# A bank copied out at once and planned durations revised in a one-core two-layer decoder kernel

## The chip, the cores and the metric

The kernel runs on one core of a Trainium2 chip. The metric is device time in microseconds (us) from launch to end of one execution; lower is better. Before the change the median of three runs is 806.67 us (804.53, 806.67, 809.62).

The engines of the core have short names: PE is the matrix engine (PEld is its weight load), DVE the vector engine, ACT the scalar engine, POOL the general-purpose engine, SP the queue that issues most of the transfers. Each engine works through its own queue in order.

## What is computed

The reference is a decoder trunk of two layers on 512 tokens of width 1024, all in float32. The change touches layer 0 alone, whose mixer is a recurrence over tokens with 16 heads of 64:

```python
xmix = xn[None] + (x_prev - xn)[None] * mu[:, None, None, :]
rkvg = jnp.einsum('cbsd,cde->cbse', xmix[:4], w_in)
...
decay = jnp.exp(-jnp.exp(-jax.nn.softplus(-w_pre) - 0.5))
a = jax.nn.sigmoid((a0 + (xa @ a1) @ a2).astype(f32))
...
kk = k * k_k.astype(f32).reshape(H, N)
kk = kk / jnp.maximum(jnp.linalg.norm(kk, axis=-1, keepdims=True), 1e-12)
k = k * (1.0 + (a - 1.0) * k_a.astype(f32).reshape(H, N))

def step(state, inp):
    r_t, w_t, k_t, v_t, kk_t, a_t = inp
    s_kk = jnp.einsum('bhij,bhj->bhi', state, kk_t)
    state = (state * w_t[:, :, None, :]
             - s_kk[..., None] * (kk_t * a_t)[:, :, None, :]
             + v_t[..., None] * k_t[:, :, None, :])
    return state, jnp.einsum('bhij,bhj->bhi', state, r_t)
```

Its output is normalised per head, gated and projected. Every layer ends with a gated embedding that is added to the residual. Layer 1 is causal differential attention with a gate, over one shared set of keys and values.

## The kernel before

**Matmuls in three passes.** Every large product is a float32 product made of three fast ones: an operand is split in a rounded high part and the rest, and `mm3` (lines 283 to 286) multiplies high by high, high by rest and rest by high. So lines 284, 285 and 286 carry all dense products. A weight tile is loaded as a pair into a RAW buffer and split in `w_split` (line 303): the rounding copy (line 269, a helper called from many places, on ACT or DVE) and the subtraction (line 317, on POOL or DVE).

**Stages of layer 0.** A dense half is a product of 1024 inputs by 512 outputs, 32 groups of three matmuls, into four PSUM banks. `ORDER` names them: r, k and v for the first half of the channels, r, k and v for the second half, half of the embedding's product p, both halves of the gate g, the rest of p. In `dense_m` the loop over the eight input tiles is the outer one and that over the four output tiles the inner one, so the four banks are taken at the first input tile and are all finished with the last. The mixed inputs are made by `mix` (lines 529 ACT, 531 DVE, 535 ACT, 537 DVE) the first time a kind is needed, and read back from DRAM the second time.

**Keys.** As an output tile i of the key half ends, `k_evac(i, pk)` (line 845) takes over its bank `pk`. It waits for `("decay", i)`, squares the bank on ACT into an H tile (line 855, for the norms), multiplies it on DVE into three operands K, A and B that the decay stage has prepared (lines 859, 861, and `scaled`, lines 722 and 725), and then gives the bank back. The norms need the squares of four tiles: `head_sums` (a product at line 812, a copy at 817, transposes at 823), the reciprocal at 833, the spread of the norms at 869 and 874. After that the operands are complete and `gram` may form its products (line 964 PE, 973 DVE).

**Decay.** `decay(i)` runs for even and odd tiles as two streams. It takes one R tile, two H tiles and banks, makes two products (lines 737 and 738), three exponentials on ACT (775, 777, 779), a running sum on DVE (771) and some merges, the last of which is on POOL (794).

**Inverse and recursion.** `inverse` solves small triangular systems by 31 steps of two DVE operations (lines 1031 and 1034), with transposes (1022, 1040, 1055), merges (1051, 1059), small copies (line 269 with 32 partitions, 1095) and small products (1067, 1081). `recur` then runs eight steps per half of the channels: products with the state (1168, 1181, 1209), half-copies of 64 x 256 elements (line 269), and the new state on DVE (1221, 1224). `finish` normalises and gates what it yields, after which the output product may start.

**What sets the order.** All these are generators that run in a planner, `Streams`, when the kernel is built. Each `yield` names an engine and a planned duration; `"ACT/DVE"` lets the planner choose the engine that ends first (a later-named one only if it ends 0.15 us earlier), a `!` means that the next step of the same stream need not wait for this one, and a `+` that the step holds a resource that DVE and POOL share in the plan. For PE a second number is the share of its columns. The planner always issues the step that can start first by its own clock, and steps of a better priority first among equals. The sequence so found is the order of every engine's queue on the chip: nothing is reordered later, and a step that is not ready holds up all behind it.

Buffers are counted too. `take` and `free` count four banks of the kind "pd" (dense products) and four of the kind "pw" (all else), 42 R tiles and 11 H tiles of SBUF, 8 weight tiles, 2 RAW buffers and 2 mixed tiles per stream. A tile of the kind H is 128 x 512 or a little more.

```python
            t = max(x[1] + lat, self.clock.get(eng, 0.0), self.port if port else 0.0)
            if best is None or t + w + PREF < best[0] + best[2]:
                best = (t, eng, w, port)
```

## Time and profile before

| what | value |
|---|---|
| median of three runs | 806.67 us |
| the profiled execution, its own time | 804.9 us |
| its span, first to last instruction | 803.1 us |
| mean granted PE clock | 0.987 |

The profile is of one execution. Its span leaves out what lies around the first and the last instruction (804.9 - 803.1 = 1.8 us). In the rows of the timeline the columns are start, length, engine, line, operation, output and inputs by the program's names, and the count of equal instructions; in brackets stands how long the engine was idle before and what released it. In rows of groups the busy time, the mean in ns and the idle time before them stand behind the bars. In rows by stretches each engine's busy time is followed by its count of instructions. A row of the waits reads: who waited, for whom, the sum in us, how often, and the longest.

### The profile page before, as it was taken

How to read it: one execution, taken by the hardware profiler on the slowest of the kernel's cores; microseconds unless marked ns; L12 is line 12 of the kernel's file. 1: busy time of each engine (PE TensorE's matmuls, PEld its weight loads, DVE VectorE, ACT ScalarE, POOL GpSimd, SP SyncE). 2: the span in 40 equal slices, each digit the busy share in tenths (PEclk: the TensorE clock that was granted, in tenths of full speed). 3: DMA queues.
4: the chain of work that ended last, by engine and by line, in shares of the span. 5: the costliest groups of instructions: out<-in, count | busy, mean ns of one | idle time of the engine just before them, and what ended most of it. 6: DMA issues, size and time to landing. Idle time of an engine off the chain costs nothing.

```text
span 803.1 us, 13885 instructions
## 1 busy us (share of the span) xinstructions
PE 757.5 (94%) x5016; PEld 605.5 (75%) x5016; DVE 590.5 (74%) x1354; ACT 453.2 (56%) x1082; POOL 200.2 (25%) x219
## 2 busy tenths in 40 slices
PE   6898899997899879999999999999999999999996
PEld 3676578876677657887778888887888878888884
DVE  2999999988759887788867675446874668835844
ACT  3789754668646555656444564333764467743431
POOL 2406405321504423886210020000000002100000
PEclk9999999999999969999999999999999999999999
DMA  8586667722326768656357434587943334224702
GB/s 322 205 277 217 226 242 267 261 92 92 120 85 227 253 215 288 196 183 198 124 171 262 131 132 134 181 302 219 289 172 105 100 85 145 85 74 157 258 6 105
DMA packets 65525, 144.60 MB, mean 180 GB/s; under 512 B 6448, under 2 KB 27184, under 8 KB 65456
## 3 DMA queue, kind: packets, MB, share of 16 engines
q1 hardware_dynamic: 42672, 108.06, 40.0%
q10 hardware_dynamic: 22784, 35.66, 12.9%
q8 instruction: 39, 0.64, 0.3%
q14 instruction: 30, 0.25, 0.1%
HBM read 105.94 MB, written 37.75 MB: 179 GB/s over the span
## 4 chain that ended last, share of the span: by engine, by line
PE 64%; DVE 17%; DMA 8%; ACT 6%; issue 3%; POOL 1%; SPq 1%; ACTq 0%; DVEq 0%; POOLq 0%
PE p L284 16%; PE p L286 15%; PE p L285 15%; PE p L1168 2%; PE p L964 2%; PE p L1768 2%; DMA RAW<-in_b_w_in 2%; DVE p L1034 2%; DVE H L1031 1%; DVE R L317 1%; PE p L1181 1%; ACT R L269 1%; DMA R<-bD 1%; PE p L1733 1%; PE p L1732 1%
## 5 line engine op out<-in xcount | busy, mean ns | idle before, releaser
L284 PE MATMUL p<-R,R 128*128 128x512 f32 x800 | 327.4, 409 | 8.4 <-ACT R L535 7.4
L285 PE MATMUL p<-R,R 128*128 128x512 f32 x800 | 314.0, 393 | 4.1 <-DVE R L537 4.1
L286 PE MATMUL p<-R,R 128*128 128x512 f32 x800 | 314.3, 393 | 0.0
L284 PEld LDWEIGHTS p<-R,R 128*128 128x128 f32 x800 | 151.2, 189 | 42.3 <-ACT R L535 9.3
L285 PEld LDWEIGHTS p<-R,R 128*128 128x128 f32 x800 | 151.5, 189 | 32.8 <-DVE R L537 6.0
L286 PEld LDWEIGHTS p<-R,R 128*128 128x128 f32 x800 | 151.0, 189 | 33.0 <-DVE R L1298 0.4
L317 POOL TENSOR_TENSOR R<-RAW,R 128x512 fp32r<-128x512 f32 x50 | 67.9, 1363 | 159.6 <-ACT R L269 86.3
L269 ACT CAST R<-RAW 128x512 fp32r<-128x512 f32 x107 | 63.9, 620 | 15.8 <-DMA RAW<-in_w_k 7.2
L317 DVE TENSOR_TENSOR R<-RAW,R 128x512 fp32r<-128x512 f32 x90 | 62.1, 704 | 12.2 <-ACT R L269 11.2
L323 DVE SCALAR_TENSOR_TENSOR R<-RAW,vec,R 128x512 fp32r<-128x512 f32 x64 | 46.5, 748 | 17.4 <-ACT R L321 16.9
L321 ACT ACTIVATE R<-RAW,vec 128x512 fp32r<-128x512 f32 x64 | 44.6, 721 | 20.2 <-DMA RAW<-in_b_w_in 12.8
L1377 POOL TENSOR_TENSOR hr<-hm,half 128x1 f32<-128x1 f32 x16 | 10.5, 656 | 147.0 <-DVE hm L1375 147.0
L1744 ACT ACTIVATE H<-p,mx 128x128 f32<-128x128 f32 (+3 forms) x64 | 33.4, 527 | 21.4 <-DVE mx L1741 20.6
L1737 DVE CUSTOM_DVE_ANT_0 p<-p,cmask 128x128 f32<-128x128 f32 (+3 forms) x64 | 30.4, 510 | 14.6 <-PE p L1733 14.4
L1034 DVE TENSOR_TENSOR p<-p,H 128x126 f32<-128x126 f32 (+22 forms) x124 | 32.6, 263 | 4.3
L280 POOL TENSOR_TENSOR orr<-orm,half 128x4 f32<-128x4 f32 x8 | 8.8, 1101 | 106.6 <-DVE orm L278 93.1
L1031 DVE TENSOR_TENSOR H<-p,R 128x126 f32<-128x126 f32 (+22 forms) x124 | 30.7, 248 | 1.1
L529 ACT ACTIVATE p<-R,omm 128x512 f32<-128x512 f32 x32 | 22.1, 692 | 13.0 <-DVE R L973 5.8
L1514 DVE SCALAR_TENSOR_TENSOR R<-H,R 128x512 f32<-128x512 f32 x16 | 11.1, 692 | 24.4 <-ACT H L1507 22.5
L1507 ACT ACTIVATE H<-p 128x512 f32<-128x512 f32 x16 | 9.5, 596 | 31.1 <-PE p L286 31.1
L1436 ACT COPY R<-p 128x512 f32<-128x512 f32 x16 | 9.4, 586 | 30.7 <-PE p L286 30.5
L1694 POOL MEMSET R<- 64x1024 f32 x8 | 7.6, 949 | 74.9 <-DMA kvD<-R 34.5
(221 smaller groups left out, 1285.1 us busy)
## 6 DMA issues: line engine op xcount, KB each, us to landing
mD<-R ACTq DMA_DIRECT2D x32, 512.0 KB, 3.9
R<-mD SPq DMA_DIRECT2D x32, 512.0 KB, 5.3
RAW<-in_ple_gate SPq DMA_DIRECT2D x16, 512.0 KB, 3.8
RAW<-in_kv_w SPq DMA_DIRECT2D x16, 512.0 KB, 3.8
RAW<-in_b_w_in SPq DMA_DIRECT2D x16, 512.0 KB, 4.3
R<-bD ACTq DMA_DIRECT2D x24, 256.0 KB, 5.6
R<-in_x SPq DMA_DIRECT2D x8, 512.0 KB, 6.1
RAW<-in_w_r SPq DMA_DIRECT2D x8, 512.0 KB, 3.8
```

The costliest lines, as they stand in the source:

```text
L269: (nc.scalar.copy if sc.eng == "ACT" else ENG[sc.eng].tensor_copy)(dst, src)
L284: nc.tensor.matmul(ps, ah, bh, start=first, stop=False)
L285: nc.tensor.matmul(ps, ah, bl, start=False, stop=False)
L286: nc.tensor.matmul(ps, al, bh, start=False, stop=last)
L317: ENG[sc.eng].tensor_sub(lo, f, hi.bitcast(F32))
L321: nc.scalar.activation(hi, f, AF.Copy, scale=g)
L323: nc.vector.scalar_tensor_tensor(lo, f, g, hi.bitcast(F32), ALU.mult, ALU.subtract)
L529: nc.scalar.activation(m, x_at(d), AF.Copy, scale=omm[:, c, d : d + 1])
L1031: ve.tensor_mul(tmp[:, 0:m, 0:w], bc(xs[:, s_ : s_ + 1, 0:w], [P, m, w]), bc(nb[:, s_ + 1 : 32, s_ : s_ + 1], [P, m, w]))
L1034: ve.tensor_add(xs[:, s_ + 1 : 32, 0:w], xs[:, s_ + 1 : 32, 0:w], tmp[:, 0:m, 0:w])
L1737: nc.vector.tensor_tensor_reduce(scs[m][:, 0:n], scs[m][:, 0:n], cmask[:, S - n : S], 1.0, -3.0e38, ALU.add, ALU.max, mx[:, m : m + 1])
L1744: nc.scalar.activation(E[m][:, 0:n], scs[m][:, 0:n], AF.Exp, bias=mx[:, m : m + 1], scale=0.125, accum_out=sm[:, m : m + 1])
```

## The change

The change edits `k_evac` and 17 planned durations. In `k_evac` the wait for the decay moves behind the square, and for the second half (tiles 4 to 7, `g == 1`) ACT copies the bank into an H tile, gives the bank back, and the three DVE operations read the copy. The other edits alter only numbers that the planner uses, and at two places the `!` of a half-copy's first part goes, which lets the plan's second part wait for the first. No priority and no count of buffers is altered.

```diff
                 if scale is None:
-                    yield "ACT/DVE+", (0.52, 0.34)
+                    yield "ACT/DVE+", (0.55, 0.45)
                     copy(hi, f)
...
-            yield "ACT", 0.57
+            yield "ACT", 0.63
             nc.scalar.activation(m, x_at(d), AF.Copy, scale=omm[:, c, d : d + 1])
...
-        yield "ACT!", 0.5
+        yield "ACT!", 0.62
         nc.scalar.activation(A, pfv[:, :, :, 0:64], AF.Exp, scale=-0.5 * DECAY)
-        yield "ACT!", 0.5
+        yield "ACT!", 0.65
         nc.scalar.activation(pf, pf, AF.Exp, scale=-0.5 * DECAY)
...
-        yield "PE", 0.95, 0.25
+        yield "PE", 1.25, 0.25
         for q in range(4):
             nc.tensor.matmul(pn[32 * q : 32 * q + 32], hsel, SQ[what, 4 * g + q], start=True, stop=True)
...
             yield "spawn", bonus(g), EVP["k"]
-        yield "wait", ("decay", i)
         yield "take", "H", 1
         sq = SQ["sq", i] = HT([P, S])
         yield "ACT", 0.57
         nc.scalar.activation(sq, pk, AF.Square, scale=vcol(V_KK, i))
         yield "set", ("sq", i)
+        if g == 1:
+            yield "take", "H", 1
+            kc = HT([P, S])
+            yield "ACT", 0.58
+            nc.scalar.copy(kc, pk)
+            yield "free", "pd", 1
+            pk = kc
+        yield "wait", ("decay", i)
         K, B, A = parts(i)
...
         scaled(i, B, v4(pk), der[:, 4, i : i + 1], B, ALU.mult)
-        yield "free", "pd", 1
+        yield ("free", "H", 1) if g == 1 else ("free", "pd", 1)
...
-                    yield "ACT/DVE+!", (0.2, 0.2)
+                    yield "ACT/DVE+!", (0.31, 0.25)
                     copy(four(na[r, 8 * u + 4 * hh : 8 * u + 4 * hh + 4]), lower(q, u, hh)[:, :, :, 32 * (q % 2) : 32 * (q % 2) + 32])
...
-        yield "PE", 1.67, 0.5
+        yield "PE", 1.15, 0.7
...
             for x in range(2):
-                yield "ACT/DVE!" if x == 0 else "ACT/DVE", (0.3, 0.35)
+                yield "ACT/DVE", (0.37, 0.4)
                 copy(tiles_of(gt, x)[HALF[par][x]], tiles_of(pA, x)[HALF[par][x]])
...
-                yield "ACT!", 0.3
+                yield "ACT!", 0.38
                 nc.scalar.copy(tiles_of(yT, x)[HALF[par][1]], tiles_of(pA, x)[HALF[par][1 - x]])
...
-        yield "Pool+", 1.0
+        yield "Pool+", 1.25
         nc.gpsimd.tensor_add(wg, wg, bc(vmean[:, cq, 8 * g : 8 * g + 8].unsqueeze(2), [P, 8, HN]))
...
-        yield "Pool+/DVE+", (1.0, 0.6)
+        yield "Pool+/DVE+", (1.25, 0.64)
         ENG[sc.eng].tensor_mul(yg, yg, bc(rs.unsqueeze(2), [P, 8, HN]))
```

The same numbers are set at the sister steps: the second small product and the copies back in `inverse`, the second pair of half-copies in `recur`, the second POOL step and the other two merges in `finish`.

More of the change, by code (lines that the diff above doesn't have):

```diff
@@ L1076, in inverse @@
         ps = [bank("pw") for _ in range(2)]
-        yield "PE", 1.67, 0.5
+        yield "PE", 1.15, 0.7
         for hd in range(16):
@@ L1087, in inverse @@
                 for q in range(4):
-                    yield "ACT/DVE+!", (0.2, 0.2)
+                    yield "ACT/DVE+!", (0.31, 0.25)
                     copy(lower(q, u, hh)[:, :, :, 32 * (q % 2) : 32 * (q % 2) + 32], four(xm[quads[q], sl]))
@@ L1199, in recur @@
             for x in range(2):
-                yield "ACT/DVE!" if x == 0 else "ACT/DVE", (0.3, 0.35)
+                yield "ACT/DVE", (0.37, 0.4)
                 copy(tiles_of(uv, x)[HALF[par][x]], tiles_of(pA, x)[HALF[par][x]])
@@ L1250, in finish @@
         bb = bon[:, cq, 4 * g : 4 * g + 4, :].rearrange("p a b -> p (a b)").unsqueeze(2)
-        yield "Pool+", 1.0
+        yield "Pool+", 1.25
         nc.gpsimd.tensor_add(wg, wg, bc(vmean[:, cq, 8 * g : 8 * g + 8].unsqueeze(2), [P, 8, HN]))
-        yield "Pool+", 1.0
+        yield "Pool+", 1.25
         nc.gpsimd.tensor_mul(wg, wg, bc(bb, [P, 8, HN]))
@@ L1266, in finish @@
         rs = yield from rsqrt(ax, s2, 1.0 / HN, GN_EPS, 8, "grs")
-        yield "Pool+/DVE+", (1.0, 0.6)
+        yield "Pool+/DVE+", (1.25, 0.64)
         ENG[sc.eng].tensor_mul(yg, yg, bc(rs.unsqueeze(2), [P, 8, HN]))
         yield "wait", ("lnxg",)
-        yield "Pool+/DVE+", (1.0, 0.6)
+        yield "Pool+/DVE+", (1.25, 0.64)
         ENG[sc.eng].tensor_mul(y, y, lnxg[0][:, gsl])
-        yield "Pool+/DVE+", (1.0, 0.6)
+        yield "Pool+/DVE+", (1.25, 0.64)
         ENG[sc.eng].tensor_add(y, y, w)
```

## The prediction

> **What bounds the kernel now.** I read the page's head and busy table first, then the table by stretches, then who waits for whom inside the poor stretches, then the timeline there. The busy table:
>
> ```profile
> span 803.1 us, 13885 instructions
> PE 757.5 (94%) x5016; PEld 605.5 (75%) x5016; DVE 590.5 (74%) x1354; ACT 453.2 (56%) x1082; POOL 200.2 (25%) x219
> PE 64%; DVE 17%; DMA 8%; ACT 6%; issue 3%; POOL 1%; SPq 1%; ACTq 0%; DVEq 0%; POOLq 0%
> ```
>
> TensorE is busy for 94% of the span and carries 64% of the chain that ended last, so what can be gained is its idle time and the time in which its clock was down. The table by stretches (length, busy time of PE, PEld, DVE, ACT and POOL, granted clock, DMA share, GB/s) tells where that is:
>
> ```profile
> core 0: us, PE busy (x) PEld busy (x) DVE busy (x) ACT busy (x) POOL busy (x), PEclk, DMA share, GB/s
> 20.00:160.00 140.00, 131.15 (x773) 99.44 (x773) 132.59 (x283) 98.56 (x203) 53.26 (x53) 1.00 0.68 243
> 184.00:216.00 32.00, 24.35 (x307) 17.99 (x306) 26.14 (x44) 24.47 (x65) 13.49 (x17) 0.95 0.34 112
> 216.00:245.00 29.00, 29.00 (x300) 22.20 (x299) 19.39 (x40) 13.81 (x38) 3.11 (x3) 1.00 0.35 112
> 245.00:275.00 30.00, 29.46 (x150) 23.60 (x150) 27.44 (x88) 19.14 (x43) 14.46 (x15) 1.00 0.78 275
> 275.00:300.00 25.00, 17.84 (x176) 13.36 (x175) 23.91 (x64) 15.20 (x41) 7.09 (x6) 0.73 0.51 185
> 300.00:420.00 120.00, 117.13 (x1087) 93.35 (x1086) 91.83 (x190) 67.14 (x168) 61.33 (x60) 1.00 0.58 195
> 420.00:803.00 383.00, 372.43 (x1845) 310.65 (x1843) 243.12 (x586) 191.45 (x474) 36.12 (x40) 1.00 0.47 154
> ```
>
> Two stretches stand out. From 184 to 216 PE is idle for 32.0 - 24.35 = 7.65 us with a clock of 0.95; from 275 to 300 it is idle for 25.0 - 17.84 = 7.16 us with a clock of 0.73. Clock loss is (1 - clock) x busy: 0.05 x 24.35 = 1.2 us and 0.27 x 17.84 = 4.8 us. Together 20.8 us. From 20 to 160 PE loses another 8.85 us in small pieces while VectorE is at 132.59 of 140; the copies are not there and I count nothing on it. After 300 PE stands at 98% and 97%, and from 216 to 245 at 100%: there nothing is to be had, and a delay there costs in full. VectorE is the second bound: 27.44 of 30 and 23.91 of 25 us between 245 and 300, but only 19.39 of 29 between 216 and 245. Inside the first stretch, PE waited for these, and these were the steps of the second half's keys (k_evac for tiles 4 to 7):
>
> ```profile
> PE p L874 <- ACT H L869: 2.2, 1, 2.2
> PE p L1181 <- DVE R L1224: 1.8, 2, 1.6
> PE p L1209 <- ACT H L754: 1.6, 1, 1.6
> PE p L1209 <- ACT R L269: 1.0, 1, 1.0
> 186.23 1.26 ACT L855 ACTIVATE H<-p,vec 128x512 f32<-128x512 f32 x2
> 204.39 0.68 ACT L855 ACTIVATE H<-p,vec 128x512 f32<-128x512 f32 x1
> 207.03 0.69 DVE L859 TENSOR_TENSOR R<-p,R 128x512 f32<-128x512 f32 x1
> 193.30 0.47 PE L284 MATMUL p<-R,R 128*128 128x512 f32 x1
> 208.84 0.47 PE L284 MATMUL p<-R,R 128*128 128x512 f32 x1
> 199.11 1.16 PE L1181 MATMUL p<-R,R 128*128 128x128 f32 x8 [1.56 <-DVE R L1224]
> 207.05 1.16 PE L1181 MATMUL p<-R,R 128*128 128x128 f32 x8 [0.28 <-DVE R L1224]
> 219.56 1.16 PE L964 MATMUL p<-R,R 64*128 64x128 f32 x16
> ```
>
> None of these waits is for the matmul stream (L284 to L286) itself; PE waits at the head of its queue for steps of the recursion and of the keys, with no matmul of the value half issued ahead of them. That half takes its four banks only as the keys' tiles give theirs back: its first matmul stands at 193.30, and groups are still scarce at 208.84. A tile gives its bank back after its three merges, and these wait for that tile's decay. The squares (L855) wait for it too: two at 186.23, the last at 204.39, which puts the key norms and so the Gram products (L964, of this half first at 219.56) behind it.
>
> **The change part by part.** *The copy of the bank* (k_evac, tiles 4 to 7). The wait for the decay moves behind the square; four copies of 128x512 from PSUM by ACT are added; three merges per tile then read SBUF; the bank goes free after the copy, and one H tile more is held until the merges are done. No DMA is moved and nothing passes SP's or POOL's queue. The prices and the matmuls of the stretch:
>
> ```profile
> L1481 ACT COPY H<-p 128x512 f32<-128x512 f32 x16 | 9.4, 589 | 9.2 <-PE p L286 9.2
> L284 PE MATMUL p<-R,R 128*128 128x512 f32 x5 | 2.4, 485 | 0.0
> L861 DVE TENSOR_TENSOR R<-p,R 128x512 f32<-128x512 f32 x4 | 2.7, 682 | 0.0
> 183.10 0.43 DVE L269 CAST R<-RAW 128x512 fp32r<-128x512 f32 x1
> 199.84 0.60 ACT L269 CAST R<-RAW 128x512 fp32r<-128x512 f32 x1
> ```
>
> The copy is the L1481 form, 589 ns, so 4 x 0.589 = 2.4 us more on ACT. ACT has 32.0 - 24.47 = 7.5 us idle in the stretch, which covers it; if the cover is gone the copies stand ahead of the recursion's small copies and cost up to 2.4 us. I take 0 and keep 0 to 2.4. The merges stay at 682 ns (L861); that they read SBUF is priced with the port below.
>
> What it brings: the banks come free after square and copy, whose four pairs take about 4 x (0.68 + 0.59) = 5 us of ACT from 186 on, so by about 191 instead of one by one until about 209. Weights are at hand: the value half's last cast before the gap stands at 183.10 and the next at 199.84, and at least three of its eight weight tiles are rounded by then (I count three), each good for four groups of three matmuls. A group takes 0.70 us (rows of the second stall below). That is 12 groups ready against 5 which ran in the stretch (L284 x5), so 7 x 0.70 = 4.9 us of matmuls can move into the 7.65 us of idle. With them goes the same share of the clock loss, 4.9 / 7.65 x 1.2 = 0.8. First term: 5.7 us. Lower end 5.7 - 2.4 = 3.3 with the copies on the path, or nothing if the time comes back later (a rival); upper end all of 8.85, since a consumed weight tile gives its buffers back and lets the next be rounded. The key norms move too, from behind 204.39 to about 191, so the 2.2 us wait of L874 for L869 should go; it lies inside the same 7.65 and isn't counted twice. What is late next is the decay of tile 7 itself, then the recursion's steps (L1181 after L1224).
>
> *The planned durations.* They issue no instruction; they change which engine a step of the slashed kind goes to and in what order all queues stand. How far the old numbers were off, and the second stall:
>
> ```profile
> L269 ACT COPY H<-R x53: 282/297/298, 99.3 to 275.9; 32x128 f32<-32x128 f32 x53
> L269 ACT CAST R<-RAW x107: 601/619/669, 19.3 to 770.7; 128x512 fp32r<-128x512 f32 x107
> L269 DVE CAST R<-RAW x33: 406/421/3389, 50.8 to 759.1; 128x512 fp32r<-128x512 f32 x33
> L529 ACT ACTIVATE p<-R,omm 128x512 f32<-128x512 f32 x32 | 22.1, 692 | 13.0 <-DVE R L973 5.8
> 276.23 0.40 PE L284 MATMUL p<-R,R 128*128 128x512 f32 x1
> 276.93 0.39 PE L284 MATMUL p<-R,R 128*128 128x512 f32 x1
> 276.29 2.08 DVE L1022 STREAM_TRANSPOSE R<-H 128x1024 f32<-128x1024 f32 x1
> 280.60 1.69 DVE L1059 TENSOR_TENSOR H<-H,unit 128x512 f32<-128x512 f32 x1
> 282.59 0.75 DVE L531 SCALAR_TENSOR_TENSOR p<-R,vec,p 128x511 f32<-128x511 f32 x1
> 284.06 0.79 PE L284 MATMUL p<-R,R 128*128 128x512 f32 x1 [5.61 <-ACT R L535]
> 278.37 5.05 POOL L317 TENSOR_TENSOR R<-RAW,R 128x512 fp32r<-128x512 f32 x3 [7.24 <-ACT R L269]
> ```
>
> The small merges of the inverse were planned at 0.20 us and took 297 ns on ACT: over these 53 alone the plan was short by 53 x 0.097 = 5.1 us. The mixing step L529 was planned at 0.57 and took 692 ns, 32 x 0.122 = 3.9 us more. Where a plan is short, an in-order queue holds a step that isn't ready ahead of one that is. The second stall looks like that: L1022 starts at 276.29, behind ACT's small copies, and L531, which PE waits for through L535 (5.61 us, row 284.06), comes only after the inverse's DVE chain at 282.59. With copies planned at 0.31 the mixing step may be put ahead. The prize is 7.16 + 4.8 = 12.0 us. But VectorE is busy there for 23.91 of 25 us, so it is only partly an error of order. From both sides: all 12.0 gone, or a second stall of the same kind elsewhere, 12.0 lost. I take a quarter, 3.0: VectorE's own idle time just before (9.6 us from 216 to 245) says that its work can move forward once the Gram products come earlier, the 96% says that not much can. The cast of a weight tile tips slightly towards ACT (0.55 against 0.45 where it was 0.52 against 0.34): 421 ns of DVE become 619 of ACT for a few of 33; nothing counted. The second half-copy of a recursion step now waits for the first in the plan, as the longer durations of the groupwise merges do theirs after 300: PE is at 98% there; nothing counted.
>
> Of this the clock bears one rule. The Trainium skill ("TensorE: Matmul & The Clock Gate", Part 1) says that an idle window of about 3.4 us halves the clock; by it only the gap of 5.61 us would cost clock time, and the gaps of the first stretch, 2.2 us at most each, would cost none, which would make the first term 4.9. The granted clock of 0.95 in that stretch speaks for a little loss there all the same.
>
> **The sum.** This profiled execution took 804.9 us (span 803.1). 804.9 - 5.7 - 3.0 = 796.2. The median of the three runs, 806.7, is 1.8 above this execution, so against the median: 798.0.
>
> **The rivals.** *The stall goes as a whole* (12.0 instead of 3.0): 806.7 - 5.7 - 12.0 = 789. For it: L531 needs nothing from the inverse. Against: VectorE at 96%. *The gain is absorbed*: the value half ends earlier and PE then stands in front of the gate half, whose operands VectorE makes at 91 to 96% load between 245 and 300; of 5.7 some 2 are left: 804.5. For it: that load. Against: 9.6 us of idle VectorE from 216 to 245 which earlier Gram products can fill. *The port*: the merges were of one PSUM and one SBUF operand, now of two in SBUF. Row 280.60 shows such an operation (L1059) at 1.69 us beside POOL's L317 (three in 5.05 us), where L861 takes 0.68, about 1.0 us more. POOL is busy for 13.49 of 32 us in the stretch, so of twelve merges some five meet it, five us of DVE, half of them on the path: 798.0 + 2.5 = 800.5. The Trainium skill ("SBUF — State Buffer", two separate sides) states the rule: a VectorE operation with two SBUF inputs and a GpSimd operation that reads SBUF lock each other out for a whole instruction; the row of L1059 agrees. *Slower: the H tiles run out.* There are 11. Four squares and four copies hold 8, the inverse 4 until its last copies, a decay 2 each. If the last two decays wait for H, the decay of tile 7 comes one recursion step later, about 8 us (L1181 runs once a step: 199.11, 207.05), the Gram products with it, and PE, which has no slack from 216 on, loses most of that: 806.7 + 6 = 813. It decides from the point at which 219.56 is not reached earlier than now. Against it: the four squares are given back at about 192 then, not after 204.39. A new order that sets a stall like that of 284.06 elsewhere costs the same kind of sum and is counted with it.
>
> **How the numbers follow.** Forecast 0.40 (own range 791 to 802, of it 0.28 below 798.6), the stall gone 0.14, absorbed 0.23, the port 0.05, H or a new stall 0.18. About 1% (8 us) is what a measurement of this kernel can tell from no change. Faster by more: 0.28 + 0.14 = 0.42; within: 0.12 + 0.23 + 0.05 = 0.40; slower: 0.18. The range 787 to 812 leaves out the best end of the stall and the larger half of the slow case.
>
> **What would show it.** Right: the second half's squares all stand within some 6 us of the end of the key matmuls; more than 5 of L284 between them and the first L964 of that half, which comes before 215; PE idle in that stretch under 4 us. The second term: a gap before L284 behind L535 of under 4 us and a clock over 0.85 there. Wrong: the copies standing ahead of the recursion's copies on ACT; merges of over 1 us beside POOL; a new gap of PE above 3 us anywhere between 20 and 420; or the first L964 no earlier than 219.

## The result and the profile after

The changed kernel takes 818.45 us in the median of four runs (814.91 to 820.14) where the kernel before takes 806.46 (804.53 to 809.62) beside it. The ratio is 1.0149, with a 95% interval of 1.0122 to 1.0176: slower, by about 12 us. The forecast was 798.0 with a range of 787 to 812, and the chance that had been given to slower was 0.18. The profiled execution of the changed kernel took 820.14 us, with a span of 818.3.

In the lines of the changed kernel, every number from 857 on is 7 higher: the square L855 is L854, since the wait ahead of it is gone, and L860 is new, the copy of the bank; L859 is L866, L964 is L971, L973 is L980, L1067 is L1074, L1181 is L1188, L1298 is L1305. The head of its page and the busy times:

```profile
span 818.3 us, 13890 instructions
PE 766.5 (94%) x5016; PEld 610.5 (75%) x5016; DVE 597.0 (73%) x1359; ACT 460.9 (56%) x1088; POOL 190.1 (23%) x212
```

These say almost nothing: the same count of matmuls, the same 94%. Three rows of the table by stretches, with the boundaries of the table before (length, busy time of PE, PEld, DVE, ACT and POOL, granted clock, DMA share, GB/s):

```profile
20.00:160.00 140.00, 128.71 (x691) 96.16 (x691) 128.97 (x264) 93.69 (x185) 53.46 (x53) 0.98 0.67 237
184.00:216.00 32.00, 23.41 (x328) 18.47 (x327) 24.08 (x43) 23.77 (x66) 9.61 (x12) 0.84 0.18 59
275.00:300.00 25.00, 15.90 (x71) 11.45 (x70) 18.44 (x49) 11.31 (x26) 3.82 (x3) 0.80 0.59 216
```

Neither poor stretch got better. From 184 to 216 PE is idle for 8.6 us (7.65 before) and its clock fell from 0.95 to 0.84; from 275 to 300 it is idle for 9.1 us (7.16 before), at a clock of 0.80 (0.73). By the prediction's own sum, idle time plus (1 - clock) x busy, the first stretch loses 12.3 us (8.9 before) and the second 12.3 (12.0). From 20 to 160, where the prediction counted nothing, PE lost 2.4 us of busy time and some clock. The timeline of the changed kernel shows what the copies did (start, length, engine, line, operation):

```profile
183.43 0.69 ACT L854 ACTIVATE H<-p,vec 128x512 f32<-128x512 f32 x1
184.53 0.59 ACT L860 COPY H<-p 128x512 f32<-128x512 f32 x1
191.97 1.25 ACT L854 ACTIVATE H<-p,vec 128x512 f32<-128x512 f32 x2
207.21 0.59 ACT L860 COPY H<-p 128x512 f32<-128x512 f32 x1
205.29 1.12 PE L1216 MATMUL p<-R,R 128*64 128x64 f32 x16 [3.59 <-ACT R L1102]
213.60 1.24 DVE L771 TENSOR_TENSOR_SCAN H<-scanm,H 128x520 f32<-128x520 f32 x1
230.71 1.16 PE L971 MATMUL p<-R,R 64*128 64x128 f32 x16
282.08 0.76 PE L284 MATMUL p<-R,R 128*128 128x512 f32 x1 [4.33 <-ACT R L535]
293.96 0.50 PE L284 MATMUL p<-R,R 128*128 128x512 f32 x1 [3.48 <-ACT R L535]
```

The squares are done at 193 instead of 205, as the change means them to be. But the copies stand at 184.53, 187.37, 195.44 and 207.21: the last bank comes free at 207.8, hardly before the 209.1 of the kernel before, and six dense groups stand between 184 and 216 where five stood. PE's longest wait there is now one of 3.59 us for copies of an inverse (L1102). The last running sum of the decays (L771) starts at 213.60, where it had started at 196.0, and the first Gram product of the second half stands at 230.71 instead of 219.56. The stall behind L535 is still there, as two waits of 4.33 and 3.48 us instead of one of 5.61. The copies cost what they had been priced at, and so did ten of the twelve merges that now read SBUF (groups of the changed kernel):

```profile
L866 DVE TENSOR_TENSOR R<-H,R 128x512 f32<-128x512 f32 x4 | 2.7, 687 | 0.5 <-ACT H L860 0.5
L860 ACT COPY H<-p 128x512 f32<-128x512 f32 x4 | 2.4, 594 | 0.0
```

The third merge of a tile, L722, took 1.67 and 1.39 us in two tiles, each time beside an operation of POOL; before, two of this line at 191.53 and 200.96 took 0.75 and 0.74:

```profile
186.40 3.01 POOL L794 TENSOR_TENSOR R<-R,H 128x512 f32<-128x512 f32 x2 [12.09 <-ACT H L779]
188.29 1.67 DVE L722 SCALAR_TENSOR_TENSOR R<-H,der,R 128x512 f32<-128x512 f32 x1
199.24 2.88 POOL L890 TENSOR_TENSOR H<-R,R 128x512 f32<-128x512 f32 x2 [0.41 <-PE p L1088]
201.27 1.39 DVE L722 SCALAR_TENSOR_TENSOR R<-H,der,R 128x512 f32<-128x512 f32 x1
```

The time is lost by *when* things run, so the useful reading is a table of milestones: the start of the first matmul of a dense group (a group is one L284 with its L285 and L286; 800 of them, numbered from 0), and of the last L1298, the last operation of `finish` on what layer 0's output product reads. All from the traces, in us, as the distance to the kernel before; the last six columns are kernels of the experiments below. Each column is one execution: that of the change was 1.7 us above its median and that of before 1.6 us below, so the last row says 15.2 where the medians differ by 12.

| milestone | before | change | bank copy alone (e1) | exponentials (e9) | head sums (e10) | change from 100 us on (e15) | change until 100 us (e16) | bank copy and head sums (e17) |
|---|---|---|---|---|---|---|---|---|
| dense group 48 | 65.8 | +5.5 | -0.6 | +9.0 | +0.2 | +1.4 | +5.0 | -0.1 |
| inverse, second batch, first product (L1067) | 174.7 | +15.9 | -0.8 | +6.4 | -0.8 | -0.4 | +9.7 | -1.3 |
| group 160, first of the value half | 193.3 | -8.1 | -6.1 | -4.0 | -13.9 | -12.4 | +1.2 | -11.6 |
| group 224 | 284.1 | +16.6 | -4.6 | +11.5 | +8.5 | -3.6 | +10.1 | -10.0 |
| last L1298 | 395.5 | +17.2 | +2.9 | +10.5 | +0.1 | +7.7 | +9.1 | +1.4 |
| last group (799) | 794.6 | +15.2 | -0.3 | +8.0 | -1.5 | +8.9 | +7.1 | +1.4 |

Behind group 352 (at 424 us) the distance no longer changes by more than 2.5 us in any of these kernels; all is decided before. Two readings matter. The value half did start 8.1 us earlier in the changed kernel, and it had turned into 16.6 us late by group 224. And the last group follows the last L1298 to within 3.2 us in every column, while it does not follow group 224 at all: e17 is 10 us ahead there and ends level, e10 is 8.5 behind and ends ahead.

### The profile page after: what moved, and what is told of

The parts are those of the page before. It is cut to its first block, busy times and chain, and to the rows that moved or that the text cites. A ratio compares the mean times of both kernels' runs of the same rounds, so it can differ in the third digit from the quotient of the medians.

```text
span 818.3 us, 13890 instructions
## 1 busy us (share of the span) xinstructions
PE 766.5 (94%) x5016; PEld 610.5 (75%) x5016; DVE 597.0 (73%) x1359; ACT 460.9 (56%) x1088; POOL 190.1 (23%) x212
## 4 chain that ended last, share of the span: by engine, by line
PE 66%; DVE 15%; DMA 8%; ACT 6%; issue 3%; POOL 1%; SPq 1%; ACTq 0%; DVEq 0%; POOLq 0%
PE p L284 16%; PE p L286 16%; PE p L285 16%; PE p L1175 3%; PE p L1775 2%; PE p L1188 2%; DMA RAW<-in_b_w_in 2%; DMA H<-in_eye 2%; DVE R L537 1%; DVE p L531 1%; DVE R L317 1%; PE p L1740 1%; PE p L971 1%; ACT R L269 1%; PE p L1739 1%
## 5 line engine op out<-in xcount | busy, mean ns | idle before, releaser
L284 PE MATMUL p<-R,R 128*128 128x512 f32 x800 | 329.5, 412 | 12.4 <-ACT R L535 8.0
L285 PE MATMUL p<-R,R 128*128 128x512 f32 x800 | 315.4, 394 | 6.3 <-DVE R L537 6.3
L286 PE MATMUL p<-R,R 128*128 128x512 f32 x800 | 315.2, 394 | 0.5 <-DVE R L1305 0.5
L284 PEld LDWEIGHTS p<-R,R 128*128 128x128 f32 x800 | 151.8, 190 | 47.5 <-ACT R L535 10.1
L285 PEld LDWEIGHTS p<-R,R 128*128 128x128 f32 x800 | 151.9, 190 | 35.3 <-DVE R L537 9.3
L286 PEld LDWEIGHTS p<-R,R 128*128 128x128 f32 x800 | 151.4, 189 | 34.4 <-DVE R L1305 1.4
L317 POOL TENSOR_TENSOR R<-RAW,R 128x512 fp32r<-128x512 f32 x53 | 70.3, 1331 | 195.5 <-ACT R L269 154.7
L269 ACT CAST R<-RAW 128x512 fp32r<-128x512 f32 x116 | 69.3, 618 | 18.8 <-DMA RAW<-in_ple_gate 5.1
L317 DVE TENSOR_TENSOR R<-RAW,R 128x512 fp32r<-128x512 f32 x87 | 62.3, 728 | 21.2 <-ACT R L269 20.1
L321 ACT ACTIVATE R<-RAW,vec 128x512 fp32r<-128x512 f32 x64 | 44.6, 720 | 19.5 <-DMA RAW<-in_b_w_in 12.4
L980 DVE TENSOR_TENSOR R<-p,cmk 128x512 f32<-128x512 f32 x32 | 21.4, 684 | 7.9 <-PE p L971 7.8
L1775 PEld LDWEIGHTS p<-R,H 128*128 128x128 f32 x160 | 22.2, 191 | 4.4 <-ACT H L1771 1.7
```

Source lines behind the costliest of these rows:

```text
L269: (nc.scalar.copy if sc.eng == "ACT" else ENG[sc.eng].tensor_copy)(dst, src)
L284: nc.tensor.matmul(ps, ah, bh, start=first, stop=False)
L285: nc.tensor.matmul(ps, ah, bl, start=False, stop=False)
L286: nc.tensor.matmul(ps, al, bh, start=False, stop=last)
L317: ENG[sc.eng].tensor_sub(lo, f, hi.bitcast(F32))
L321: nc.scalar.activation(hi, f, AF.Copy, scale=g)
```

## The experiments

The theories. T1: the edit of k_evac costs the time. T2: the planned durations do, since they set another order. T3: only both together. T4: one number is to blame. T5: any new order costs as much. T6 and T7 came up after the second set, T8 and T9 after the third.

| kernel | what differs from before | median, us | ratio (95% interval) | PE clock, 60 to 75 us |
|---|---|---|---|---|
| the change | | 818.45 | 1.0149 (1.0122 to 1.0176) | 0.77 |
| e1 | k_evac alone | 804.86 | 0.9986 (0.9967 to 1.0005) | 1.00 |
| e2 | planned durations alone | 822.62 | 1.0205 (1.0163 to 1.0247) | 0.89 |
| e3 | half-copies alone | 816.19 | 1.0116 (1.0071 to 1.0162) | 1.00 |
| e4 | all but the half-copies | 829.46 | 1.0275 (1.0233 to 1.0316) | 0.77 |
| e5 | cast and mixing | 812.00 | 1.0093 (1.0057 to 1.0130) | 0.89 |
| e6 | exponentials, head sums | 822.53 | 1.0227 (1.0189 to 1.0265) | 0.77 |
| e7 | inverse | 809.42 | 1.0048 (1.0026 to 1.0070) | 1.00 |
| e8 | a number without meaning | 804.65 | 0.9979 (0.9955 to 1.0004) | 1.00 |
| e9 | exponentials | 814.34 | 1.0105 (1.0066 to 1.0144) | 0.66 |
| e10 | head sums | 803.30 | 0.9962 (0.9941 to 0.9984) | 1.00 |
| e11 | exponentials, shorter | 820.34 | 1.0173 (1.0139 to 1.0206) | 0.89 |
| e12 | start-to-start times | 815.21 | 1.0109 (1.0079 to 1.0139) | 0.89 |
| e13 | delay in tile 0's decay | 808.94 | 1.0042 (1.0018 to 1.0066) | 0.77 |
| e14 | delay in tile 6's decay | 808.46 | 1.0034 (1.0013 to 1.0056) | 1.00 |
| e15 | the change from 100 us on | 812.35 | 1.0079 (1.0050 to 1.0108) | 1.00 |
| e16 | the durations until 100 us | 813.08 | 1.0095 (1.0068 to 1.0121) | 0.89 |
| e17 | k_evac and head sums | 808.66 | 1.0046 (1.0031 to 1.0060) | 1.00 |

**First set: which half of the change.** e1 has the two hunks in `k_evac` (the moved wait, the copy, the exchanged `free`) and all numbers of before. e2 has all 17 numbers and the two marks and the old `k_evac`. e3 and e4 split off the half-copies of the recursion:

```diff
-                yield "ACT/DVE!" if x == 0 else "ACT/DVE", (0.3, 0.35)
+                yield "ACT/DVE", (0.37, 0.4)
...
-                yield "ACT!", 0.3
+                yield "ACT!", 0.38
```

> Only the edit of k_evac (square before the wait, copy of the second half's banks), all planned durations as before. In the changed kernel the last running sum of the decay stage starts 17.6 us later than before (213.6 against 196.0) and the second small product of the inverse's second batch 19.4 us later. Theory 1: the early squares, copies and norm steps of tiles 4 to 6 take H tiles and banks of the kind pw ahead of tile 7's decay and of the inverse, so this edit alone is slow: 814 to 820 us, last running sum after 208. Theory 2: the planned durations shift the order and this edit alone is harmless or a gain: 800 to 807 us, last running sum before 200. Theory 3, only both together are slow: within 1% of before.

> All 17 planned durations and the two dropped marks, k_evac as before. Theory 1 expects 804 to 809 us, as before. Theory 2 expects 814 to 822 us, with the 5 us that the first Gram product is late (96.6 against 91.3) and most of the delay of the recursion. Theory 3: within 1% of before. The 5 us at the first Gram product should be here under every theory, since nothing is copied in the first half.

> Of the durations only those of recur: the half-copies at 0.37 and 0.40 without the mark on the first one, and the copies of its result at 0.38. No bank copy. If the recursion's new plan is what is slow, this costs at least half of the 12 us: 812 us or more. If the loss is of the bank copy or of the other durations: 804 to 809 us.

> The whole change without these three edits of recur. If they are the cause, back to 800 to 808 us. If not, 814 to 822 us as with the whole change.

e1 measured 0.9986, e2 1.0205, e3 1.0116, e4 1.0275. T1 falls and so does T3: the loss is there with the durations alone. T2 holds, with e2 0.6 us above its range; but its second sign does not come, since the last running sum of e1 starts at 204.3 and not before 200. The half-copies cost 1.2% alone, and yet the change is *worse* without them, outside both ranges of e4, so parts do not add up.

The trace of e1 shows what became of the first term of the prediction. Two stretches of e1 that are needed here, the first stretch of the prediction, and a row of PE's waits in it:

```profile
184.00:216.00 32.00, 27.62 (x273) 20.23 (x274) 23.55 (x43) 23.75 (x58) 10.36 (x15) 0.84 0.29 102
PE p L284 <- ACT H L860: 3.3, 2, 1.8
200.00:240.00 40.00, 39.92 (x488) 31.70 (x488) 30.74 (x61) 25.21 (x67) 9.12 (x13) 1.00 0.37 120
280.00:320.00 40.00, 33.95 (x359) 25.85 (x357) 35.34 (x98) 25.40 (x63) 8.64 (x11) 0.79 0.56 199
```

The two stretches before, and one that is needed below:

```profile
200.00:240.00 40.00, 36.54 (x428) 27.13 (x427) 28.29 (x53) 22.78 (x62) 12.37 (x15) 1.00 0.30 96
280.00:320.00 40.00, 33.52 (x436) 25.76 (x438) 33.38 (x93) 21.25 (x59) 12.08 (x15) 0.83 0.68 240
360.00:400.00 40.00, 39.22 (x279) 30.85 (x278) 34.17 (x69) 22.20 (x51) 19.92 (x18) 1.00 0.51 167
```

From 200 to 240 PE gains 3.4 us of busy time, as meant, and from 184 to 216 twelve dense groups stand, as the prediction had counted, where five stood. But PE now waits at the head of its queue for the copies themselves (L284 behind L860, 3.3 us in two waits), and its clock is at 0.5 from 187.5 to 197.7. By the prediction's sum the stretch from 184 to 216 loses 4.4 + 4.4 = 8.8 us in e1, where it lost 8.9. From 280 to 320 PE stands as before, at a lower clock. Dense products were brought forward, but not the work that layer 0 ends with: the seven products with the state (L1181) of the recursion's second half stand 2.6 to 9.8 us later.

**Second set: which number.** Each of the first three has some of the change's numbers: e5 those of the cast and the mixing step, e6 those of the two exponentials and the head sums, e7 those of the inverse's small copies and products:

```diff
-                    yield "ACT/DVE+", (0.52, 0.34)
+                    yield "ACT/DVE+", (0.55, 0.45)
...
-        yield "ACT!", 0.5
+        yield "ACT!", 0.62
...
-        yield "PE", 1.67, 0.5
+        yield "PE", 1.15, 0.7
```

One line of each of the three stands here. e8 moves a number that stands for nothing:

```diff
-    LATENCY = {"DMA": 2.4, "PE": 0.2, "ACT": 0.14, "DVE": 0.13, "Pool": 0.09}
+    LATENCY = {"DMA": 2.4, "PE": 0.2, "ACT": 0.14, "DVE": 0.135, "Pool": 0.09}
```

> Only two numbers: the weight cast at (0.55, 0.45) and the first step of the mixing at 0.63. With all durations together the second key tile's groups at 65.8 come 4.7 us later than before (first Gram product 4.5 later); with the half-copies alone 0.4. Theory 4, one number is to blame: one of the groups of this set of runs carries that delay and 8 us or more by itself, the others stay within 804 to 809. Theory 5, any new order costs about as much, whichever number makes it: each of these runs is at 808 to 820 us, the one with the meaningless edit too, with delays in different places.

> Only the two exponentials of the decay at 0.62 and 0.65 and the head sums at 1.25. Theory 4: if these are to blame, first Gram product 4 us later and 814 us or more; else 804 to 809. Theory 5: 808 to 820.

> Only the inverse's small copies at (0.31, 0.25) and its small products at 1.15 with a share of 0.7. Nothing can change before the first inverse, so the first Gram product stays at 91 under both theories. Theory 4: if these are to blame, the second batch's products (174.7 before, 11.7 later with all durations) are late by 8 us or more and the time is 814 or more; else 804 to 809, or below if the stall at 284 goes. Theory 5: 808 to 820.

> No duration is touched; the planner's allowance between the end of a DVE step and its use is 0.135 instead of 0.13, a number that stands for nothing measured. Theory 4: 804 to 808 us, as before. Theory 5: a new order that costs like the others, 810 to 820 us.

Measured: 1.0093, 1.0227, 1.0048 and 0.9979. e6 alone costs as much as all numbers together, which speaks for T4. The four parts (e3, e5, e6, e7) add up to 4.8% against 2.05% for e2; the numbers of `finish` were not run alone. e8 costs nothing, so T5 falls in its strong form: not every new order is slow. Its order is that of before until about 100 us, so it says nothing of what an early reordering costs.

**Third set: is it the size of the number?** Rows of the timeline of the kernel before, three instructions of ACT that follow one another without a pause:

```profile
58.79 0.62 ACT L777 ACTIVATE R<-H 128x512 f32<-128x512 f32 x1
59.44 0.64 ACT L779 ACTIVATE H<-H 128x520 f32<-128x520 f32 x1
59.98 1.06 ACT L535 CAST R<-p 128x512 fp32r<-128x512 f32 x2
```

L779 lasts 0.64 us, but the next instruction starts 59.98 - 59.44 = 0.54 us after it: these neighbours overlap by 0.1 us. The change plans L779 at 0.65, its length; the plan before had 0.5. From such rows came T6: lengths as planned numbers count the overlap twice. Its rival T7: any move of the number gives another order, and the loss depends on that order and not on the sign. e9 and e10 split e6: e9 has the change's two lines of the exponentials, e10 its line of the head sums. e11 moves the exponentials downward by 0.12:

```diff
-        yield "ACT!", 0.5
+        yield "ACT!", 0.38
...
-        yield "ACT!", 0.5
+        yield "ACT!", 0.38
```

e12 sets the numbers to start-to-start times, these among them:

```diff
-        yield "ACT!", 0.5
+        yield "ACT!", 0.52
...
-        yield "ACT!", 0.5
+        yield "ACT!", 0.54
...
-                    yield "ACT/DVE+!", (0.2, 0.2)
+                    yield "ACT/DVE+!", (0.27, 0.13)
...
-                yield "ACT/DVE!" if x == 0 else "ACT/DVE", (0.3, 0.35)
+                yield "ACT/DVE!" if x == 0 else "ACT/DVE", (0.27, 0.34)
```

For the small copies and the half-copies, e12's 0.27 on ACT is not the time from start to start where they follow one another. In the kernel before five small copies of 0.297 us take 1.52 us, and two half-copies of 0.37 us take 0.74; they do not overlap there:

```profile
99.34 1.52 ACT L269 COPY H<-R 32x128 f32<-32x128 f32 x5
200.47 0.74 ACT L269 COPY H<-p 64x256 f32<-64x256 f32 x2
```

So e12 tests start-to-start times for the exponentials and the mixing, but not for these copies; the two steps of `finish` that only POOL can take stay at 1.0.

> Of the whole change only the two exponentials of the decay, planned at 0.62 and 0.65 instead of 0.5 and 0.5. Together with the head sums they gave 1.023 of the time before. T4 (one of the two kinds of number carries it; the exponentials, because seven decays run twice over them and each feeds a Gram): 818 to 826 us, and the inverse's products of the second batch 5 us or more later than before. Rival T4b (the head sums carry it): 803 to 808. Third (neither alone: the loss needs both): both this and the next under 810.

> Of the whole change only the PE head sums, planned at 1.25 instead of 0.95, for 4 groups of 8 matmuls in the whole kernel. T4 (exponentials carry it): 803 to 808 us. T4b (the head sums carry it): 818 to 826. Third (the loss needs both): under 810.

> The two exponentials planned at 0.38 instead of 0.5, an error of the same size as the change's but downward. T6 (the planner loses because the new number counts the overlap of neighbouring instructions twice and so books ACT too full): an error downward does not book ACT too full, 802 to 810 us. Rival T7 (any move of this number by 0.12 reorders the decays' ACT steps, and the loss depends on the order that falls out and not on the sign): as likely slow as not, 810 us or more counts for it. It cannot exclude T7 if it comes out fast.

> All the durations that the change touches, set not to the durations in the profile of before but to the time from the start of one instruction to the start of the next where they stand back to back in it: casts 0.52 and 0.34 (as before), mixing 0.63, exponentials 0.52 and 0.54, small copies 0.27 and 0.13, inverse products 1.15 with share 0.7, half-copies 0.27 and 0.34 (their marks as before), the copy behind the output 0.27, merges on POOL 1.25; head sums as before. T6 (the durations of the change count the overlap of about 0.1 us of neighbouring instructions twice): 800 to 808 us, against 822.6 with the change's numbers. T7 (any other set of numbers gives another order and most orders are worse): 810 to 825.

Measured: 1.0105, 0.9962, 1.0173 and 1.0109. Shortening the exponentials costs more than lengthening them, and e12's numbers cost 1.1%. T6 falls, by e11 above all, which it had put at 802 to 810; T7 stands. T4 had put e9 at 818 to 826 and falls too. e10 is the one kernel with its whole interval below 1, by 0.2 to 0.6%; as one of eighteen intervals that is weak evidence. That the exponentials cost 1.05% and the head sums gain 0.4%, and both together cost 2.3%, says again that no number carries a fixed price.

**Fourth set: where the loss starts.** The last column of the table divides the kernels: ten show a PE clock below 1.00 between 60 and 75 us, and all ten have their interval above 1; of the eight others (and the kernel before) two lose more than half a per cent, e3 and e15, and three lose 0.3 to 0.5%, e7, e14 and e17. T8 is that this early wait and the clock lost behind it are the first cause of the loss; T9, that the wait only goes along with a loss that comes from the order behind 100 us. What happens there, in the timeline of the changed kernel:

```profile
54.41 1.41 POOL L317 TENSOR_TENSOR R<-RAW,R 128x512 fp32r<-128x512 f32 x1 [1.49 <-DVE R L269]
54.58 3.47 DVE L771 TENSOR_TENSOR_SCAN H<-scanm,H 128x520 f32<-128x520 f32 x2
59.53 1.20 POOL L794 TENSOR_TENSOR R<-R,H 128x512 f32<-128x512 f32 x1 [3.71 <-ACT H L779]
59.86 1.19 DVE L269 CAST R<-RAW 128x512 fp32r<-128x512 f32 x1
61.09 0.69 DVE L317 TENSOR_TENSOR R<-RAW,R 128x512 fp32r<-128x512 f32 x1
61.70 0.68 DVE L788 TENSOR_TENSOR R<-H,p 128x512 f32<-128x512 f32 x1
62.43 0.50 PE L737 MATMUL p<-R,R 128*128 128x512 f32 x1 [1.73 <-DVE R L788]
63.70 0.79 PE L737 MATMUL p<-R,R 128*128 128x512 f32 x1 [0.53 <-DVE R L537]
```

And in that of the kernel before:

```profile
53.37 1.24 DVE L771 TENSOR_TENSOR_SCAN H<-scanm,H 128x520 f32<-128x520 f32 x1
56.16 1.24 DVE L771 TENSOR_TENSOR_SCAN H<-scanm,H 128x520 f32<-128x520 f32 x1
59.66 0.68 DVE L788 TENSOR_TENSOR R<-H,p 128x512 f32<-128x512 f32 x1
60.49 0.47 PE L737 MATMUL p<-R,R 128*128 128x512 f32 x1 [0.46 <-DVE R L788]
```

In the changed order two running sums take 3.47 us instead of 2.48, the first of them beside a subtraction on POOL, and end 0.65 us later than before. Ahead of L788 there now stand a cast, which takes 1.19 us beside POOL's L794, and a subtraction, so L788 starts 2.04 us later. The decay's product L737 at the head of PE's queue waits 1.73 us for it with dense groups queued behind (and the next one 0.53 us), and the clock goes to 0.5 from 63.7 to 70.5. Other kernels of the ten come to such a wait in other ways (in e9 both sums take 1.23). To see what the wait itself costs, e13 makes it in the order of before, number for number, with three products on DVE that the plan does not know; e14 does the same at tile 6. e15 and e16 give the change to one part of the run:

```diff
+        if i == 0:
+            for _ in range(3):
+                nc.vector.tensor_mul(K, v4(ta), v4(ta))
         pfv = pf.rearrange("p (a b) j -> p a b j", b=2)
...
-        yield "ACT!", 0.5
+        yield ("ACT!", 0.62) if sc.clock.get("PE", 0.0) < 100.0 else ("ACT!", 0.5)
```

The first hunk is e13 (e14 has `i == 6`); the second shows the form in which e16, and e15 with the two sides exchanged, have every number; e15 has the new `k_evac` too.

> The order of before, number for number, with three extra 128x512 products on DVE (about 1.8 us by the start-to-start of 0.60) in the decay of tile 0 behind its running sum, of which the plan knows nothing; what they write is overwritten. It makes the early wait alone. T8 (the early wait and the clock lost behind it are the first cause of the loss): PE waits about 2 us at 60 to 62, the clock is at 0.5 behind it, group 48 is 4 us late or more, and the run takes 811 to 818 us. Rival T9 (the wait only goes along with the loss, which comes from the order behind 100 us): group 48 late, but the run within 804 to 809, as the later stalls of the same order swallow it.

> As e13, the three extra products in the decay of tile 6 instead, which lies at about 184 us. T8: the chain from decay to Gram to inverse to state steps has little slack there, the end is 1 to 5 us later, 807 to 811 us. T9's view of the order as a thing with slack in it: 804 to 807.

> The whole change, but with the numbers of before until PE's planned clock is 100 us, and so the order of before until about there: the bank copy and the numbers of the change work in the part behind. T8: 800 to 809 us. T9: 811 to 822.

> The numbers of the change until PE's planned clock is 100 us, those of before behind it, no bank copy. T8: the early wait is there (group 48 late by 4 to 6 us) and the run takes 811 to 820 us. T9: 803 to 809.

Measured: 1.0042, 1.0034, 1.0079 and 1.0095. In the timeline of e13 the three products and the wait that they make:

```profile
55.49 2.12 DVE L774 TENSOR_TENSOR R<-H 128x512 f32<-128x512 f32 x3
64.39 0.76 PE L737 MATMUL p<-R,R 128*128 128x512 f32 x1 [3.18 <-DVE R L791]
```

From 60 to 75 us, by stretches, in the kernel before:

```profile
60.00:75.00 15.00, 13.51 (x57) 10.34 (x56) 14.29 (x23) 14.02 (x28) 8.35 (x8) 1.00 0.63 221
```

in the changed kernel:

```profile
60.00:75.00 15.00, 11.75 (x38) 8.34 (x37) 13.57 (x20) 12.09 (x23) 5.36 (x7) 0.77 0.55 204
```

and in e13:

```profile
60.00:75.00 15.00, 11.67 (x38) 8.57 (x37) 13.77 (x23) 11.71 (x23) 5.21 (x6) 0.77 0.67 244
```

e13 reproduces the early picture of the change: 38 matmuls instead of 57 in these 15 us, a clock of 0.77, group 48 late by 6.1 us. Some 1.3 us of that lies ahead of the change, at the start of the run, as e14 and e15 show, whose order up to there is that of before (+1.2 and +1.4). So about 2 us of work on DVE became nearly 5 us of delay of the dense products. Of that the run loses 0.18 to 0.66%, 1.5 to 5.3 us. The median, 808.94, lies in T9's range and not in T8's, though the group is as late as T8 said. Of the other three, e14 and e16 lie in T8's ranges and e15 in T9's. So the early wait costs, but less than e16 loses, and T8 holds in part only: the order behind it costs too. e15 shows T9's side, as its early part is that of before and it still loses 0.8%. By place the losses come near to adding up: 0.95% until 100 us and 0.79% behind make 1.74%, against 1.49% for the change (1.22 to 1.76). The order behind 100 us is not the same in e15 as in the change, so this may be luck; that a loss starts in either part is shown, the shares are not.

What e15 loses can be read by stretches:

```profile
200.00:240.00 40.00, 39.61 (x454) 31.00 (x455) 28.75 (x61) 20.85 (x57) 9.77 (x14) 1.00 0.33 107
360.00:400.00 40.00, 34.85 (x285) 26.32 (x280) 32.39 (x59) 18.97 (x46) 21.23 (x19) 0.96 0.34 105
```

PE has 3.1 us more of work done from 200 to 240 than before and 4.4 us less from 360 to 400. Of its waits from 360 to 420 (who for whom, sum, how often, longest) these are for the merges of `finish`:

```profile
PE p L1291 <- POOL R L1280: 2.0, 1, 2.0
PE p L1291 <- DVE R L1280: 1.3, 1, 1.3
```

L1291 holds the transposes of what `finish` has merged (L1280). In between, the recursion's second to seventh product with the state (L1181, here L1188) of the first half stand 11.6 to 26.4 us later in e15 than before, but that lateness does not reach the end: the products of the second half stand 1.3, 0.4 and 0.2 us later, then 5.0, 7.9, 7.6 and 7.4, and the last L1298 7.7. The third and the fifth, in e15:

```profile
328.57 1.16 PE L1188 MATMUL p<-R,R 128*128 128x128 f32 x8
356.69 1.16 PE L1188 MATMUL p<-R,R 128*128 128x128 f32 x8
320.00:360.00 40.00, 40.00 (x480) 32.04 (x481) 36.45 (x74) 27.87 (x73) 24.58 (x25) 1.00 0.66 216
```

In the kernel before they stand at 328.36 and 348.81. PE has no idle time here. Between the two products stand 24 dense groups where 16 stood, and eight groups of some 0.70 us are 5.6 of the 7.7 us. So dense groups had gone ahead of the chain from the recursion to the last L1298. That one caused the other is read from the trace; no run isolates it.

**Fifth: the parts that cost nothing, together.** e17 has the two hunks in `k_evac` and, of the numbers, the head sums.

> The bank copy of the change with the head sums planned at 1.25, all else as before: the two parts of the change that cost nothing alone. If the effects were additive: 0.9986 times 0.9962, about 802 us and faster than the kernel before. T7 (each set of numbers gives an order of its own, whose time does not follow from the parts): anything from 800 to 815, and more than 806 counts for it.

Measured: 1.0046, where the product of the two would have been 0.995. T7 again. The stretch in which its lead goes:

```profile
360.00:400.00 40.00, 34.76 (x252) 26.83 (x251) 32.17 (x64) 16.57 (x40) 15.94 (x12) 0.95 0.42 135
```

It has the largest lead of all at group 224, 10 us, and gives it back in the same place, 34.76 against 39.22 of 40 us from 360 to 400. Among the kernels run here only e10, which leaves k_evac as it was, measures faster than the kernel before beyond its interval, by 0.4%.

## Why the prediction was wrong, step by step

- **The planned durations ("I take a quarter, 3.0").** This is the step that failed, in sign and size. They were read as a correction of an error that had been seen at one stall, L531 behind the inverse's DVE chain, and a gain was booked for it. What they did is reorder every queue from the first 50 us on; alone they cost 2.05% (1.63 to 2.47), about 16.5 us, instead of bringing 3.0. That a number nearer to a length on the chip gives a better order was the unspoken assumption: e11 (further away) and e12 (start-to-start times for the exponentials) both lose as well, so the nearness of the number does not decide.
- **"From 20 to 160 ... I count nothing on it".** The copies are not there, but the casts, the mixing step and the exponentials are, and their numbers change. e16 puts 0.95% (0.68 to 1.21) there, with a PE clock of 0.89 from 60 to 75 us.
- **The first term, 5.7 us for the copy of the bank.** With the numbers of before the mechanism is right and the value is not. In e1 all four copies stand between 186.5 and 192.1, twelve groups run as counted, and the value half starts 6.1 us earlier. But the new waits of PE for the copies and the clock of 0.84 take the time back in the same stretch (8.8 us lost against 8.9), and the run gains between -0.4 and +2.7 us (e1's interval). PE's idle time there was also priced as time on the path that sets the end, and that path runs through the last L1298, which does not come earlier (+2.9). The rival "the gain is absorbed" describes e1, though at another place: not in front of the gate half. In the change the new order leaves even the mechanism half done: the value half starts 8.1 us earlier, but the fourth copy stands at 207.21 and not at 191.
- **The costs of the copy** were right as lengths, 594 ns each, taken from a row of 589. That other idle time of ACT covers them was not: in e1 PE waits 3.3 us for them, where 0 to 2.4 had been kept, and the clock falls behind the first of these waits.
- **The wait of L874 for L869** was put down to the late squares. In the kernel before, a cast of 3.39 us stands in DVE's queue between two steps of the key norms (L831 and L833), beside POOL's L883; the casts of this kind take 421 ns in the middle:

```profile
206.99 4.98 POOL L883 TENSOR_TENSOR H<-R,R 128x512 f32<-128x512 f32 x4
209.11 3.39 DVE L269 CAST R<-RAW 128x512 fp32r<-128x512 f32 x1
```

- **The port, as a rival,** came about on two of the twelve merges of the change (1.67 and 1.39 us) and on three of e1 (1.51 and 1.68 us, and 1.65 for a half), where five had been counted; the others stayed at their price. Whether the end waits for any of it is not shown. It was also at work 130 us earlier, in the running sum beside POOL's subtraction.
- **Slower, as a rival.** Its sign came: the first Gram product was not earlier than 219.56 but at 230.71, and the last decay was late, its running sum by 8.3 us in e1 and 17.6 in the change. Yet in e1 that lateness costs the run nothing, so it is not the cause by itself; whether H tiles or banks held that decay up was not tried. The "new stall elsewhere" that was counted with it is nearer to what happened, at 60 us in the change and from 360 on in e15 and e17, and had too small a chance. The 813 that was worked out for this rival lies 6 us above the kernel before, less than the 8 us that the prediction says can be told from no change.
- **The second stall "may" lose L531's delay.** It stayed: 7.8 us behind L535 in the changed kernel (4.33 and 3.48) against 5.61.
- **The range** ended at 812. It took the worst case as one stall's worth; a reordering of all queues can make several.

## What to carry to other kernels

Planned durations in a list scheduler are not a model that gets better with each number set right: a change of any of them is a new order, to be timed as such, and here nine of eleven sets of numbers without the bank copy were slower by more than their interval. Before booking idle time of the busiest engine as a gain, find the last operation that the next stage waits for (here the last normalised output) and ask whether it moves; dense work done earlier is worth nothing when the chain behind it is not. And look for the first place where a reordered queue holds a step that is not ready: about 2 us of delay in one decay made dense products nearly 5 us late, by the wait and by the clock behind it.

## What the runs showed of the hardware beyond that

- Neighbouring instructions on ACT and DVE can overlap. In the trace of before, where they stand back to back, start-to-start times of these are about 0.1 us below the lengths: casts on ACT 521 against 620 ns, on DVE 336 against 422, L317 on DVE 602 against 686. A sum of lengths overstates what an engine needs for them. Small copies of 32 partitions on ACT that follow one another (L269) do not overlap: 308 ns from start to start against a length of 297.
- A running sum (L771) takes 1.24 us alone and 2.22 to 2.35 where POOL's subtraction L317 was running already as it began. Where the sum began first (kernel before, at 66.19, the subtraction at 66.41), it took 1.23 and the subtraction 2.09 instead of some 1.3.
- The clock falls without any long gap. In the changed kernel it goes to 0.5 at 63.7; in the 3.4 us before, PE waited 1.73 us once and some 0.5 us again. The Trainium skill ("TensorE: Matmul & The Clock Gate", Part 1) speaks of an idle window of about 3.4 us; by that the wait of 1.73 us would have cost no clock, and the trace disagrees. In the kernel before, a wait of 1.78 us at 74.6 left the clock at 1.00, so how the wait lies in time matters as well. In each of the 19 traces all changes of the clock lie whole multiples of 3.41 us apart. Counted back in such steps from the fall at 188.3 of the kernel before, a border at 75.7 cuts that wait, and the two steps hold 1.0 and 1.1 us of idle PE; the step from 60.3 to 63.7 of the changed kernel holds 2.26. In these traces no step at full clock with more than 1.92 us of idle PE was followed by another one at full clock; some falls came behind less, down to 0.96.
